# Interleaving input tiles and weight blocks one to one at the start of an eight-core hybrid layer

## The chip, the cores and the metric

The kernel runs on all 8 cores of one Trainium2 chip; each core does one prompt of 2048 tokens and 16 single-token samples. The metric is the device time in microseconds (us) of the slowest core, as the median of several executions. Some executions fall into a slower state in which the cores of one die show a lower granted TensorE clock (in the changed kernel's run of 851.31 us, 0.876 to 0.912 on the cores of one die and 0.985 to 0.995 on those of the other); they are left out.

Because the slowest core varies from run to run, I also use the mean span of the eight cores over the timed fast runs ("mean core"), and, from the profiled execution of each kernel, a count that I call **lost TensorE time**: time t minus the full-clock lengths of all matmuls that TensorE has started by t, averaged over the eight cores. The full-clock length is put at 0.4167 ns a column + 2.5 ns. That line gives 55.8, 145.8 and 215.8 ns for the bf16 matmuls of 128, 344 and 512 columns; in the trace of the kernel before the median distance between the starts of two of them is 56, 146 and 216 ns (396 of 344 columns take 57.77 us of its chain, 145.9 ns each, at a granted clock of 1.00). Matmuls of 16 columns come out too short: they start 25 ns apart in bf16 and 62 in fp32, where the count has 9 and 29; at the measured distances the gain of the change by 70 us would be 8.6 us instead of the 9.9 below, and the gain by 100 us the same 7.2. I counted the few fp32 matmuls with four times their columns, which is an assumption. That is too long for the fp32 ones of 128 columns, which start 109 ns apart in the trace, about twice the 56 of the bf16 ones; counted so, the rows of the tables rise by up to 2.4 us, but the gains of the change over the kernel before move by at most 0.5 us. A curve of lost time is worked out by me from the trace and isn't a view of the profile; tables marked "lost" hold it.

## The reference

```python
u = rmsnorm(x, norm_g)
lx, lg, sb, scg, sh, sg, q, qg, mg = split(u @ w_in)       # 1024 -> 8704 columns
xc = causal_dwconv4(lx) + b;  hs = rglru(xc)               # gated linear recurrence
z_a = (hs * silu(lg)) @ lru_wo
z_b = (silu(sg) * sb * causal_dwconv3(scg * sh)) @ sconv_wo
z_c = (attention(q, memory_k, memory_v) * silu(qg)) @ xa_wo
y   = x + (sigmoid(mg_a)*z_a + sigmoid(mg_b)*z_b + sigmoid(mg_c)*z_c) @ w_out
out = rmsnorm(y)             # and new states, memory keys and values
```

## The kernel before

The program isn't written in execution order. It builds a graph of tasks, and a planner at build time plays the tasks through with assumed durations and transfer times. That play fixes the order of the instructions on every engine, and the list is kept on the chip: on core 0 of the kernel before, ScalarE idles 10.57 us until 46.97 us over one evacuation, although the tiles that come next on its list had all landed by 41.3 us (the last was asked for at 25.1 us, and none took over 16.2 us). So an assumption in the planner never makes anything faster by itself, but it decides what stands behind what.

The parts that matter (cuts are marked with `# ...`):

```python
# an input tile of 128 tokens: load, square sum on ScalarE, 1/rms on GpSimd,
# scaling on VectorE (even tiles) or GpSimd (odd tiles), 8 transposes on TensorE, gain on VectorE
def p0(ti, src, nr, dst, gcols, tdst, prio):
    G.dma("sp", [(lambda: x_.ap[0:nr, :], src)], nr * 4096, [], [x_.tok], prio, None)
    G.act(... Square, accum_out=stat ...)
    rstd(ti, nr, prio)                       # two small GpSimd instructions
    # ... scale on DVE or Pool
    G.pe([tr(kc) for kc in range(KC)], 0.65, [xn_.tok, m_identb.t], [ps.tok], prio)
    G.dve(... dst = psum * gain ...)
for i in range(17):
    p0(i, src, nr, uT[:, :, i * 128:i * 128 + nr], pT[:, 0:8], t_uT[i], -100 + i)
for i in range(2):
    p0(17 + i, memp[...], ...)               # memory tokens
params()                                     # six small loads, early priority

# a weight block: 1024 x 128 columns, cast to bf16 by the DMA, issued by GpSimd
def wload(ap, prio):
    hw = Handle(w2ring if 2 <= state["nw"] < 6 else wring)
    t = G.dma("pool", [...], k * 65536 * 1.18, [], [hw.tok], prio, None)
    if state["nw"] >= 2:
        G.after(t, t_rs[min(16, state["nw"] + 1)])    # after the 1/rms of a tile
    state["nw"] += 1

# a projection of one block: 3 units of 688 columns, 16 matmuls of 344 columns each
def unit(lhs, nk, rhs, u, reads, prio, hold=()):
    G.pe([mm(k, b) for k in range(nk) for b in range(2)], ...)

# in the planner's play of a DMA
a, n = max(dmafree[q], end + 0.8), t.dma[1] / 250e3
fin = dmafree[q] + 1.3
# and among ready tasks: those within 0.4 us of the earliest compete by priority
```

A unit of 688 columns needs input tiles 0 to 5 (unit 0), 5 to 10 (unit 1), or 10 to 16 (unit 2).

The softmax here doesn't subtract the row's maximum and nothing guards it: scores larger than these inputs give would overflow.

## Time and profile before

| | before |
|---|---|
| median time | 781.86 us (three runs, 780.9 to 782.59) |
| mean core span | 777.5 us |
| TensorE busy | 93% of the span |

The first lines are from the page of the slowest core (core 0): busy time and instructions by engine, then busy tenths in 40 slices of 19.5 us, and the shares of the chain that ended last.

```profile
PE 726.6 (93%) x4884; PEld 460.6 (59%) x4884; DVE 395.2 (51%) x379; ACT 340.2 (44%) x404; POOL 247.5 (32%) x303
...
PE   2579998999999998999999999999999999999995
...
PEclk9979998999999999999999999999999999999998
DMA  8999921414242333242334595655896828226933
...
PE 85%; DMA 5%; issue 2%; ACT 2%; DVE 2%; POOL 2%; SPq 0%; POOLq 0%; ACTq 0%; DVEq 0%
```

TensorE (PE) is nearly full from the fourth slice on. The first three slices aren't, and the DMA engines (last row) are busiest there: the start is a phase of its own, bound by transfers, and the rest is bound by TensorE.

The DMA queues between 12 and 16 us (queue, packets, MB, share of the 16 engines): q1 carries the input tiles, q0 the weights.

```profile
q1 hardware_dynamic: 294, 1.08, 85.8%
q0 software_dynamic: 292, 0.07, 20.9%
```

The two queues send the same number of packets. A tile's packet is 4 KB, a weight's is 256 B as written, so the weights get about a sixteenth of the bytes (0.07 MB against 1.08). A block of 256 KB has 1024 packets and a tile of 512 KB 128: at equal counts one block lands per eight tiles. That the queues take turns packet by packet is my reading of the equal counts (294 and 292 here, 337 and 338 between 24 and 28 us); more than the counts the trace doesn't show.

What that does to the engines, on core 0. In the chain (start, length, what), and then by engine in order of time (start, length, engine, line, instruction, and in brackets the idle time before it with its releaser):

```profile
18.23 23.49 DMA R<-w_in
```

```profile
24.49 4.03 PE L761 MATMUL PP<-R 128*128 128x344 bf16 x16 [1.48 <-DVE R L674]
...
32.03 2.49 PE L761 MATMUL PP<-R 128*128 128x344 bf16 x16 [2.11 <-DMA R<-w_in]
...
42.13 4.75 PE L761 MATMUL PP<-R 128*128 128x344 bf16 x16 [7.16 <-DMA R<-w_in]
```

```profile
46.97 0.73 ACT L936 CAST R<-PP 128x688 bf16<-128x688 f32 x1 [10.57 <-PE PP L761]
```

```profile
38.22 0.95 POOL L133 DMA_DIRECT2D R<-w_in  x1
48.91 0.18 POOL L651 TENSOR_SCALAR R<-R 128x1 f32<-128x1 f32 x1 [9.75 <-ACT R L734]
...
51.70 0.96 POOL L133 DMA_DIRECT2D R<-w_in  x1
```

The third block, asked for at 18.23 us, arrives only when TensorE can start at 42.13. That stalls a convoy: ScalarE has the evacuation of that unit next in its list and idles 10.57 us; the row statistics of the next tiles stand behind it; GpSimd waits 9.75 us for those; and GpSimd is also the engine that asks for weight blocks, so none is asked for between 38.22 and 51.70 us. (The named releaser, line 734, is ScalarE's small parameter work just behind the statistics, which ended at 48.74.)

Lastly the projection matmuls alone, by stretch (stretch, its length, busy us and count, granted clock, DMA share, GB/s); the clock column reads 1.00 before the first clock record, though eight transposes take 1.01 us there and 0.61 us later:

```profile
core 0: us, PE busy (x), PEclk, DMA share, GB/s
0.00:40.00 40.00, 6.52 (x32) 0.97 0.98 259
40.00:50.00 10.00, 6.48 (x28) 0.59 1.26 114
50.00:70.00 20.00, 11.39 (x77) 1.00 0.83 89
70.00:100.00 30.00, 29.75 (x202) 1.00 1.02 116
100.00:140.00 40.00, 23.78 (x143) 0.91 0.22 41
140.00:360.00 220.00, 195.26 (x1310) 0.99 0.35 33
```

By 70 us core 0 has done 32 + 28 + 77 = 137 of 4104 projection matmuls, 20 us of work.

### The profile page before, as it was taken

What the parts mean: (1) busy time and instruction counts of PE and PEld (TensorE: products, weight loads), DVE (VectorE), ACT (ScalarE), POOL (GpSimd) and SP (SyncE); (2) the same over time, 40 slices, a digit from 0 to 9 for tenths busy, and PEclk for the clock granted to TensorE, in tenths of its full rate; (3) what the DMA queues carried; (4) which work ended last, traced back from release to release, by engine and by line L of the source; (5) the groups of instructions that cost most, each with busy time, mean ns of one, the idle gap of its engine ahead of it and who ended that gap; (6) DMA issues with size and microseconds to landing.
All of it is one profiled execution on the core that took longest, in us unless ns stands there. A gap on an engine that the chain in (4) does not pass through costs nothing.

```text
span 782.0 us, 13246 instructions; the slowest of 8 cores (776.0 to 782.0 us)
## 1 busy us (share of the span) xinstructions
PE 726.6 (93%) x4884; PEld 460.6 (59%) x4884; DVE 395.2 (51%) x379; ACT 340.2 (44%) x404; POOL 247.5 (32%) x303
## 2 busy tenths in 40 slices
PE   2579998999999998999999999999999999999995
PEld 1356654655655654666666666666666666665442
DVE  3544043265684863877875874546321221223665
ACT  4442358886759658676571211121212112112332
POOL 5845000121120210212114344435464454423221
PEclk9979998999999999999999999999999999999998
DMA  8999921414242333242334595655896828226933
GB/s 223 296 92 129 117 68 15 41 15 41 28 45 25 28 34 35 28 41 24 39 31 78 81 194 88 94 110 66 111 121 73 119 28 76 23 109 215 294 141 138
DMA packets 112618, 69.47 MB, mean 89 GB/s; under 512 B 93987, under 2 KB 100213, under 8 KB 112539
## 3 DMA queue, kind: packets, MB, share of 16 engines
q0 software_dynamic: 99808, 31.60, 39.3%
q1 hardware_dynamic: 12747, 37.03, 14.4%
q8 instruction: 40, 0.66, 0.4%
q14 instruction: 23, 0.19, 0.1%
HBM read 90.53 MB, written 9.82 MB: 128 GB/s over the span
## 4 chain that ended last, share of the span: by engine, by line
PE 85%; DMA 5%; issue 2%; ACT 2%; DVE 2%; POOL 2%; SPq 0%; POOLq 0%; ACTq 0%; DVEq 0%
PE PP L761 73%; PE PP L1189 8%; DMA R<-w_in 3%; PE PP L967 2%; DMA R<-xp 1%; PE PP L901 1%; ACT R L825 1%; PE PP L959 1%; DMA R<-cv 1%; POOL R L653 1%; PE PP L1053 1%; DVE R L839 1%; ACT R L962 1%; POOL R L663 0%; DVE R L1072 0%
## 5 line engine op out<-in xcount | busy, mean ns | idle before, releaser
L761 PE MATMUL PP<-R 128*128 128x344 bf16 x4104 | 616.5, 311 | 17.2 <-DMA R<-w_in 9.3
L761 PEld LDWEIGHTS PP<-R 128*128 128x128 bf16 x4104 | 400.1, 98 | 225.9 <-issue 28.2
L133 POOL DMA_DIRECT2D R<-w_in x68 | 61.7, 910 | 293.0 <-PE PP L761 266.3
L1141 ACT ACTIVATE R<-PP 128x688 f32<-128x688 f32 x72 | 53.6, 744 | 221.8 <-PE PP L761 197.8
L1150 DVE SCALAR_TENSOR_TENSOR R<-R,PP 128x688 f32<-128x688 f32 x72 | 62.5, 871 | 157.3 <-PE PP L761 134.5
L1189 PE MATMUL PP<-R 128*128 128x512 bf16 (+1 forms) x272 | 59.0, 379 | 0.0
L1154 POOL TENSOR_TENSOR R<-R 128x688 f32<-128x688 f32 x24 | 39.3, 1642 | 33.5 <-DVE R L1150 32.5
L812 DVE SCALAR_TENSOR_TENSOR R<-R 128x2048 f32<-128x2048 f32 x18 | 42.3, 2349 | 8.1 <-ACT R L809 7.0
L1189 PEld LDWEIGHTS PP<-R 128*128 128x128 bf16 (+1 forms) x272 | 26.4, 97 | 32.2 <-issue 0.4
L1159 POOL TENSOR_TENSOR R<-R 128x688 bf16<-128x688 f32 x24 | 38.9, 1642 | 17.7 <-DVE R L1150 17.5
L1198 ACT ACTIVATE R<-R 128x1024 f32<-128x1024 f32 (+1 forms) x17 | 18.0, 1057 | 46.3 <-DVE R L1193 46.3
L867 DVE TENSOR_TENSOR R<-PP,R 128x688 f32<-128x688 f32 x18 | 15.7, 874 | 31.0 <-PE PP L761 31.0
L1193 DVE SCALAR_TENSOR_TENSOR R<-PP,R 128x1024 f32<-128x1024 f32 (+1 forms) x17 | 20.8, 1224 | 20.6 <-PE PP L1189 20.6
L825 ACT ACTIVATE R<-PP,R 128x688 f32<-128x688 f32 x36 | 27.7, 833 | 6.4 <-PE PP L761 6.4
L674 DVE TENSOR_TENSOR R<-PP,R 128x1024 bf16<-128x1024 bf16 (+1 forms) x19 | 21.6, 1171 | 17.0 <-PE PP L671 16.5
L671 PE MATMUL PP<-R 128*128 128x128 bf16 (+1 forms) x152 | 13.7, 252 | 16.5 <-DVE R L663 12.7
L873 DVE SCALAR_TENSOR_TENSOR R<-R 128x2048 f32<-128x2048 f32 x12 | 28.2, 2347 | 0.9 <-ACT R L870 0.7
L651 POOL TENSOR_SCALAR R<-R 128x1 f32<-128x1 f32 (+1 forms) x36 | 7.5, 209 | 62.5 <-ACT R L1198 44.5
L839 DVE TENSOR_TENSOR_SCAN R<-R 128x2048 f32<-128x2048 f32 x6 | 26.5, 4422 | 0.4
L975 DVE TENSOR_TENSOR R<-PP,R 128x512 f32<-128x512 f32 x16 | 10.9, 688 | 29.3 <-ACT R L973 21.4
L1055 DVE TENSOR_TENSOR R<-R,PP 128x1024 f32<-128x1024 f32 x16 | 19.5, 1216 | 11.2 <-PE PP L1053 9.4
L936 ACT CAST R<-PP 128x688 bf16<-128x688 f32 x12 | 8.8, 730 | 35.1 <-PE PP L761 33.5
(129 smaller groups left out, 587.9 us busy)
## 6 DMA issues: line engine op xcount, KB each, us to landing
R<-w_in POOLq DMA_DIRECT2D x68, 256.0 KB, 5.1
R<-xp SPq DMA_DIRECT2D x32, 512.0 KB, 9.1
R<-ck SPq DMA_DIRECT2D x16, 512.0 KB, 4.2
y_p<-R SPq DMA_DIRECT2D x16, 512.0 KB, 2.8
R<-cv POOLq DMA_DIRECT2D x16, 256.0 KB, 7.2
R<-w_out POOLq DMA_DIRECT2D x8, 256.0 KB, 6.4
R<-xa_wo POOLq DMA_DIRECT2D x14, 128.0 KB, 4.1
R<-lru_wo POOLq DMA_DIRECT2D x8, 192.0 KB, 4.6
```

The costliest lines, as they stand in the source:

```text
L133: eng.dma_start(out=out, in_=in_).then_inc(sems[semkey], 16)
L674: G.dve(lambda e: e.tensor_tensor(out=dst, in0=ps.ap.bitcast(BF16)[:, 0:1024].rearrange("p (k t) -> p k t", k=KC)[:, :, 0:nr], in1=gcols.u ...
L761: return lambda e: e.matmul(ps.ap[:, b * 512:b * 512 + BLK], lhs(k), rhs[:, k, c:c + BLK], start=(k == 0), stop=(k == nk - 1))
L812: G.dve(lambda e, k=k: e.scalar_tensor_tensor(out=xc[:, 0:T], in0=lxp[:, k:k + T], scalar=cw(k), in1=xc[:, 0:T], op0=ALU.mult, op1=ALU.add ...
L825: G.act(lambda e, ps=ps, dst=dst, u=u, bcol=bcol: e.activation(out=cols(dst, u), in_=pv(ps), func=AF.Tanh, scale=0.5, bias=dv[:, bcol:bcol ...
L839: G.dve(lambda e: e.tensor_tensor_scan(out=xc[:, 0:T], data0=thr[:, 0:T], data1=thi[:, 0:T], initial=0.0, op0=ALU.mult, op1=ALU.add), T, t ...
L873: G.dve(lambda e, k=k: e.scalar_tensor_tensor(out=cy[:, 0:T], in0=cinp[:, k:k + T], scalar=sw(k), in1=cy[:, 0:T], op0=ALU.mult, op1=ALU.ad ...
L1141: G.act(lambda e, ps=pg[u], th_=th_: e.activation(out=b3(th_.ap), in_=pv(ps), func=AF.Tanh, scale=0.5), UW, [pg[u].tok], [th_.tok], Px - E ...
L1150: G.dve(lambda e, zp=zp, th_=th_, dst=dst: e.scalar_tensor_tensor(out=b3(dst.ap), in0=b3(th_.ap), scalar=1.0, in1=pv(zp), op0=ALU.add, op1 ...
L1154: G.pool(lambda e, acc=acc, th_=th_: e.tensor_tensor(out=acc.ap, in0=acc.ap, in1=th_.ap, op=ALU.add), 1.6, [acc.tok, th_.tok], [acc.tok], Px)
L1159: G.pool(lambda e, acc=acc, th_=th_, u=u, j=j: e.tensor_tensor(out=mT[:, j, u * UW:(u + 1) * UW], in0=acc.ap, in1=th_.ap, op=ALU.add), 1.6 ...
L1189: return lambda e: e.matmul(ps.ap[0:nr, b * 512:(b + 1) * 512], mT[:, k, c0:c0 + nr], wo[:, k, b * 512:(b + 1) * 512], start=(k == 0), sto ...
```

## The change

Its intent: let tiles and weights share the DMA engines evenly, so that TensorE finds work from the first tiles on. The core of the diff (moved code and priorities of the small parameter work are cut):

```diff
+def wload(ap, prio):                       # no longer tied to a tile's 1/rms, but:
+    if "pre" in state:
+        G.after(G.tasks[-1], state["pre"])  # behind the list of first blocks
+def unit(..., split=False):                 # start of the kernel: halves of 344 columns
+    if split:
+        for b in range(2):
+            t = G.pe([mm(k, b) for k in range(nk)], ...)
+            t.xgate = [t_tr[i] for i in range(17) if i * 128 < (u + 1) * UW] if b == 0 else []
+first = [C_Q, C_Q + 128, C_Q + 256, C_Q + 384, C_LG, C_SG, C_LX, C_SB, C_LG + 128, C_SCG, C_SH, C_SG + 128, C_LX + 128]
 for i in range(17):
+    if i >= 6:
+        wait = [w_toks[min(i - 5, len(w_toks) - 1)]]   # a tile waits for a weight block
+    elif i >= 3:
+        wait = [x_toks[i - 3]]                         # at most three tiles in flight
+    else:
+        wait = []
-    p0(i, src, nr, uT[...], pT[:, 0:8], t_uT[i], -100 + i)
+    x_toks.append(p0(i, src, nr, uT[...], pT[:, 0:8], t_uT[i], -100 + i, wait))
+    while len(w_toks) < len(first) and len(w_toks) <= i:
+        hw, lhs = wload(w_in_cols(first[len(w_toks)]), -100 + i)   # block i with tile i
+        if len(w_toks) >= 1:
+            G.after(G.tasks[-1], t_rs[i])
 # parameter and state loads: priority -88 -> 20 and -87 -> 25, after tiles 10 and 15
 # memory tokens: after the last block of the list
-        kv(pos)
+        kv(pos + KVP)                        # KVP = 10
-            if n < 4:
-                step(attend, n, d=14)
+            if 1 <= n < 5:
+                step(attend, n - 1, d=14)    # attention one gate stage later
-                sample_values(P - 5, 1.5)
+                sample_values(P - 5, 2.5)
 # planner: 250 -> 240 KB per us, landing 1.3 -> 2.3 us, tie window 0.4 -> 0.3 us
```

## The prediction

> **What bounds the kernel now.** TensorE: 726.6 of 782.0 us busy (the profile's first part), and the chain that ended last is 85% PE. A warm 128x344 matmul costs 146 ns (timeline). What is left is TensorE idling or running cold, and the table by windows puts most of it at the start. Up to 69.1 us TensorE did 128 projection matmuls (18.7 us warm), 152 input transposes (11.6 us at 76 ns) and the state transposes (2.3 us): 32.6 us of work, so about 36 us are lost. From 69 us on only some 16 us are idle in the whole run, plus about 8 us of output after the last matmul.
>
> **Why the start loses.** The chain shows one link of 23.5 us, "DMA R<-w_in": the third weight block, asked for at 18.2 us, lands after 41 us. The DMA view by 4 us windows shows the reason: while input tiles (4 KB packets, hardware queue) are queued, the weight queue (256 B packets) sends exactly as many packets: 294 against 292 in 12 to 16 us, 337 against 338 in 24 to 28 us. [...] A block has 1024 packets, a tile 128, so one block lands per eight tiles. Alone, a block needs about 1.9 us (2118 packets in 40 to 44 us). TensorE stands idle or at half clock from 34.9 to 46 us.
>
> **What the change does.** No work is removed. At most three tiles are in flight, and from the sixth on a tile waits for a weight block, so the weights get the engines. Estimated from the rates above: a tile 1.6 us, a block 1.9 us, a pair 3.5 us. First two blocks at about 15 and 17 us (seven or so blocks by 35 us; before, about two), tile 10 at about 33, the last tile at about 54 us (later than before, about 40), block 13 at about 55 us. First projection matmul at about 19 us (before 24.5). From 19 to 37 us TensorE gets a third-block (2.3 us) and a tile's transposes (0.6 us) per pair; from about 38 us, when tiles 6 to 10 are in, it has a backlog and should not idle until past 70 us. Loss in the start: 15 us ideally, 20 with cold matmuls and order errors: 16 us saved of the 36.
>
> Moved too: parameter and state loads come later, off the path. Attention shifts one gate stage later, so its stalls (122 to 133 us, ScalarE) move to later stages instead of vanishing. Keys and values: neutral. Wider spacing of the sample values: 1 to 2 us of the 557 to 576 us gap on this core, less on others.
>
> All saved start time lies on the critical path, as TensorE is nearly full afterwards. Minus 16 to 20 us, given back 1 to 2: about 764 us.
>
> **Predicted: 764 us**, 80% range 755 to 776. Faster by over 2% (under 766.2): 0.57; within 2%: 0.39; slower: 0.04.
>
> **What would show it.** Hardware packets well below software packets from 15 to 50 us; median weight landing in the start far under 20 us; no idle of TensorE over 4 us after 20 us; lost TensorE time in the first 70 us 15 to 22 us; from 140 us on the table by windows alike except shifted.
>
> **What would make it wrong.** TensorE's fixed order, planned from assumed transfer times, blocks on a late block or tile; evacuations wait for buffers shared with input tiles; the last tile's lateness; new attention and gate collisions.

## The result, and the profile after

| | before | after |
|---|---|---|
| median time | 781.61 us (4 runs) | 778.57 us (3 fast runs 777.24 to 779.0; a slow one of 851.31 left out) |
| ratio of the fast runs | | 0.9956 (95% interval 0.9936 to 0.9977) |
| mean core span | 777.5 us | 772.3 us |

A ratio is the mean time of one kernel's fast runs over that of the other's of the same rounds, so it isn't quite the ratio of the medians. The change is worth 0.4% of the slowest core and 0.7% of the mean core; 764 us had been forecast, with a range up to 776.

The page of the slowest core (core 4), the same rows as before:

```profile
PE 727.6 (94%) x4884; PEld 459.4 (59%) x4884; DVE 398.3 (51%) x379; ACT 344.8 (44%) x408; POOL 246.0 (32%) x303
...
PE   2887999989999989989999999999999999999995
...
PEclk9999999999999989989999999999999999999998
DMA  9998934422613322412333694655895848226833
```

The second slice of TensorE rose from 5 to 8, the third from 7 to 8; the fourth fell from 9 to 7. The dip has moved. The DMA queues between 24 and 28 us now:

```profile
q0 software_dynamic: 992, 0.25, 70.1%
q1 hardware_dynamic: 144, 0.52, 40.8%
```

Weights send seven times as many packets as tiles, where before they sent as many. Median time from issue to landing of a weight block: 8.4 us (core 4, the first 80 us) instead of 19.9 (core 0, the first 110 us). So the mechanism that the change aims at works. The first projection matmuls and then the place near 66 us, on TensorE:

```profile
24.50 9.51 PE L644 MATMUL PP<-R 128*128 128x344 bf16 x56
```

```profile
61.38 1.33 PE L644 MATMUL PP<-R 128*128 128x344 bf16 x8
66.40 0.61 PE L710 MATMUL PP<-R 128*128 128x128 bf16 x8 [3.69 <-POOL R L702]
66.85 3.66 PE L644 MATMUL PP<-R 128*128 128x344 bf16 x24
```

The first projection matmul starts at 24.50 us, as before (24.49), and at 66.40 TensorE has been idle for 3.69 us until a late input tile (line 710 is the transposes) is scaled. The chain shows the same two queues taking turns as the limit:

```profile
43.25 13.61 DMA R<-w_in
...
57.08 5.38 DMA R<-xp
```

The projection matmuls by stretch on core 4:

```profile
core 4: us, PE busy (x), PEclk, DMA share, GB/s
0.00:40.00 40.00, 13.69 (x83) 1.00 0.99 193
40.00:50.00 10.00, 8.89 (x60) 1.00 1.21 183
50.00:70.00 20.00, 12.72 (x84) 1.00 0.95 184
70.00:100.00 30.00, 24.22 (x148) 0.94 1.10 128
100.00:140.00 40.00, 33.50 (x228) 1.00 0.37 54
140.00:360.00 220.00, 186.24 (x1219) 0.97 0.33 31
```

Up to 50 us core 4 has done 143 of them, against 60 in the kernel before. Up to 70 us it is 227 against 137. But from 70 to 100 us it does only 148, against 202. (In that stretch it also has to do the state transposes and the memory keys and values, which the kernel before has partly behind it or still ahead.) Lost TensorE time, in which those other matmuls are counted as work:

| lost by (us) | 20 | 40 | 50 | 70 | 100 | 140 | 200 | 280 | 360 | 760 |
|---|---|---|---|---|---|---|---|---|---|---|
| before | 18.2 | 30.7 | 34.4 | 40.6 | 41.8 | 46.2 | 50.0 | 52.4 | 58.3 | 67.2 |
| after | 18.2 | 24.1 | 24.8 | 30.7 | 34.6 | 34.6 | 39.3 | 48.0 | 53.3 | 62.9 |
| gain | 0 | 6.6 | 9.6 | 9.9 | 7.2 | 11.6 | 10.7 | 4.4 | 5.0 | 4.3 |

So nothing is gained in the first 20 us, 9.6 us in the next 30, and some of it is given back twice: between 70 and 100 us, and between 200 and 280 us. (The 11.6 at 140 is a loan: the kernel before has its first attention stall at 120 to 140 us, the changed one has it later.)

Spans and granted clock of the fastest and slowest core, before and then after:

```profile
core 0: 782.0 us, clock 0.983
...
core 2: 776.0 us, clock 0.992
```

```profile
core 0: 770.2 us, clock 0.997
...
core 4: 777.0 us, clock 0.985
```

In these two runs the fastest core has a higher granted clock than the slowest, with the same instructions (0.992 against 0.983, 0.997 against 0.985). In the profiled run after, core 0 has no half-clock spell between its warm-up and the end, and core 4 has 17 us of them (granted clock 0.5). In such a spell 16 matmuls of 344 columns took 4.75 us (core 0 of the kernel before, from 42.13 us), and 2.49 us before it (from 32.03 us). Half clock for 17 us is an estimated 8.5 us of lost work, more than the 6.8 us between the two cores. The metric takes the unluckiest of eight.

### The profile page after: what moved, and what is told of

Same layout as the page of the kernel before. It is cut to its first block, busy times and chain, and to the rows that moved or that the text cites. A ratio compares the mean times of both kernels' runs of the same rounds, so it can differ in the third digit from the quotient of the medians.

```text
span 777.0 us, 13244 instructions; the slowest of 8 cores (770.2 to 777.0 us)
## 1 busy us (share of the span) xinstructions
PE 727.6 (94%) x4884; PEld 459.4 (59%) x4884; DVE 398.3 (51%) x379; ACT 344.8 (44%) x408; POOL 246.0 (32%) x303
## 4 chain that ended last, share of the span: by engine, by line
PE 84%; DMA 6%; ACT 3%; DVE 2%; issue 2%; POOL 1%; POOLq 0%; SPq 0%; ACTq 0%; DVEq 0%
PE PP L644 72%; PE PP L1211 8%; DMA R<-xp 3%; DMA R<-w_in 3%; PE PP L989 2%; ACT R L847 1%; PE PP L981 1%; DVE R L834 1%; PE PP L1075 1%; ACT R L984 1%; PE PP L1114 0%; POOL R L692 0%; POOL R L702 0%; ACT R L698 0%; PE PP L770 0%
## 5 line engine op out<-in xcount | busy, mean ns | idle before, releaser
L644 PEld LDWEIGHTS PP<-R 128*128 128x128 bf16 x4104 | 399.4, 98 | 216.1 <-issue 19.4
L1172 DVE SCALAR_TENSOR_TENSOR R<-R,PP 128x688 f32<-128x688 f32 x72 | 62.6, 871 | 151.1 <-PE PP L644 137.0
L1176 POOL TENSOR_TENSOR R<-R 128x688 f32<-128x688 f32 x24 | 39.4, 1641 | 36.8 <-DVE R L1172 35.9
L1211 PEld LDWEIGHTS PP<-R 128*128 128x128 bf16 (+1 forms) x272 | 26.4, 97 | 32.3 <-issue 0.4
L713 DVE TENSOR_TENSOR R<-PP,R 128x1024 bf16<-128x1024 bf16 (+1 forms) x19 | 22.3, 1175 | 23.2 <-PE PP L710 21.7
L847 ACT ACTIVATE R<-PP,R 128x688 f32<-128x688 f32 x36 | 27.4, 834 | 5.0 <-PE PP L644 4.9
L895 DVE SCALAR_TENSOR_TENSOR R<-R 128x2048 f32<-128x2048 f32 x12 | 28.2, 2346 | 0.9 <-ACT R L892 0.7
L698 ACT ACTIVATE R<-R 128x1024 bf16<-128x1024 f32 (+1 forms) x19 | 20.1, 1056 | 15.9 <-DMA R<-xp 15.7
L710 PEld LDWEIGHTS PP<-R 128*128 128x128 bf16 (+1 forms) x152 | 10.8, 110 | 25.6 <-issue 25.1
```

The costliest lines, as they stand in the source:

```text
L644: return lambda e: e.matmul(ps.ap[:, b * 512:b * 512 + BLK], lhs(k), rhs[:, k, c:c + BLK], start=(k == 0), stop=(k == nk - 1))
L710: return lambda e: e.transpose(ps.ap.bitcast(BF16)[:, kc * 128:kc * 128 + nr], xn_.ap[0:nr, kc * 128:(kc + 1) * 128], identb[0:nr, 0:nr])
L847: G.act(lambda e, ps=ps, dst=dst, u=u, bcol=bcol: e.activation(out=cols(dst, u), in_=pv(ps), func=AF.Tanh, scale=0.5, bias=dv[:, bcol:bcol ...
L895: G.dve(lambda e, k=k: e.scalar_tensor_tensor(out=cy[:, 0:T], in0=cinp[:, k:k + T], scalar=sw(k), in1=cy[:, 0:T], op0=ALU.mult, op1=ALU.ad ...
L1172: G.dve(lambda e, zp=zp, th_=th_, dst=dst: e.scalar_tensor_tensor(out=b3(dst.ap), in0=b3(th_.ap), scalar=1.0, in1=pv(zp), op0=ALU.add, op1 ...
L1176: G.pool(lambda e, acc=acc, th_=th_: e.tensor_tensor(out=acc.ap, in0=acc.ap, in1=th_.ap, op=ALU.add), 1.6, [acc.tok, th_.tok], [acc.tok], Px)
```

## The experiments

Each kernel is the changed kernel with one edit unless it says otherwise; all gave correct results, all were timed over five rounds beside the kernel before. The changed kernel itself was not timed again in these rounds: its figures are the three fast runs of the first session, and the kernel before, which stayed within 777.3 to 777.7 us, is what ties the sessions together. Lost time is from the profiled execution, the mean core and the median from the timed fast runs.

| run | lost by 40 | 50 | 70 | 100 | 360 | 760 | mean core | median | ratio to before |
|---|---|---|---|---|---|---|---|---|---|
| before | 30.7 | 34.4 | 40.6 | 41.8 | 58.3 | 67.2 | 777.5 | 781.6 | 1 |
| after | 24.1 | 24.8 | 30.7 | 34.6 | 53.3 | 62.9 | 772.3 | 778.6 | 0.9956 |
| e1 attention back | 24.4 | 25.4 | 31.3 | 35.5 | 55.6 | 64.5 | 773.5 | 777.8 | 0.9946 |
| e3 no tile waits | 31.2 | 31.6 | 34.1 | 35.9 | 55.1 | 64.5 | 776.7 | 780.5 | 1.0003 |
| e4 tie window | 23.9 | 25.4 | 32.9 | 37.6 | 58.8 | 68.8 | 777.1 | 780.9 | 0.9994 |
| e5 slower DMA in the plan | 23.3 | 26.0 | 30.8 | 35.1 | 51.5 | 61.2 | 771.0 | 774.7 | 0.9914 |
| e6 two tiles per block | 24.4 | 27.4 | 29.7 | 33.4 | 54.4 | 63.7 | 773.2 | 778.2 | 0.9953 |
| e7 parameters early | 24.4 | 25.5 | 30.6 | 34.3 | 52.1 | 61.6 | 772.0 | 776.3 | 0.9937 |
| e8 whole units | 25.6 | 28.2 | 31.0 | 34.3 | 54.4 | 63.8 | 772.9 | 778.4 | 0.9959 |
| e9 before, new plan numbers | 31.1 | 34.1 | 37.8 | 39.5 | 56.7 | 66.6 | 778.0 | 783.3 | 1.0025 |
| e10 first half unit early | 22.3 | 25.6 | 29.3 | 32.0 | 49.1 | 59.2 | 768.8 | 773.6 | 0.9900 |
| e11 keys, values back | 24.4 | 25.5 | 32.1 | 36.5 | 54.3 | 64.4 | 773.9 | 780.1 | 0.9991 |
| e12 state transposes spread | 24.7 | 25.7 | 31.5 | 35.4 | 55.2 | 64.5 | 773.6 | 777.4 | 0.9951 |
| e13 combined | 22.4 | 26.8 | 30.0 | 33.9 | 50.4 | 60.1 | 769.6 | 774.4 | 0.9910 |
| e14 list ahead alone | 30.2 | 31.7 | 33.4 | 35.8 | 52.4 | 62.3 | 773.3 | 778.8 | 0.9968 |
| e15 e10 without tile waits | 31.1 | 32.3 | 34.1 | 37.1 | 57.0 | 66.3 | 777.0 | 781.2 | 1.0006 |
| e16 two half units early | 21.9 | 25.1 | 29.4 | 33.2 | 50.8 | 60.9 | 769.4 | 773.1 | 0.9895 |

### How far the planned order alone moves the time (e4)

```diff
-                    if r <= m + 0.3:
+                    if r <= m + 0.4:
```

> A control: the changed kernel with only the tie window of its planner put back from 0.3 to 0.4 us, so that the order of many instructions differs for no physical reason. If the order alone decides a few us (rival to every one-part explanation here), the time moves by 3 us or more either way; if not, it stays within 2 us of 778.8. Its own plan is 4 us longer than that of the changed kernel, so 780 to 784 if the chip follows the plan.

Measured: the mean core rises by 4.8 us, the median by 2.3. Nothing physical was changed, so an edit anywhere in this kernel can move the mean core by some 5 us (this is one control; others might move it more) merely because the planner deals the instructions in another order. A difference of one or two us between two rows of the table is therefore no evidence for a cause; the rows are read by where their lost time parts, and by the trace at that place.

### The tile waits taken away (e3)

```diff
-            if i >= 6:   wait = [w_toks[min(i - 5, len(w_toks) - 1)]]
-            elif i >= 3: wait = [x_toks[i - 3]]
-            else:        wait = []
+            wait = []
```

> The changed kernel with all waits of input tiles on other tiles or weight blocks taken away, so that tiles are queued as early as their buffers allow; all else as changed. If packets of the two queues taken in turn are what starved the weights, the third to sixth weight blocks land about 20 us after their issue again (8.4 us in the changed kernel), hardware and software packets are equal in number from 12 to 36 us, TensorE idles 5 us or more in one piece before 50 us and the time is 782 to 790 us. Rival (the alternation is not what gained; the later parameter and state loads or the halved units are): within 2 us of the changed kernel's 778.8.

Measured: the packets are equal in number again. Between 24 and 28 us:

```profile
q1 hardware_dynamic: 305, 1.12, 84.0%
q0 software_dynamic: 306, 0.08, 25.9%
```

The median landing of a block is 22.2 us, TensorE idles 5.4 to 6.6 us in one piece before 34 us on every core, and by 40 us 31.2 us are lost, 7.1 more than in the changed kernel. So the starvation is real and the alternation removes it. But by 100 us the two kernels are 1.3 us apart. Without the waits all tiles are in early, the blocks then come with nothing beside them (from 40 to 44 us the weight queue sends 1077 packets and the tile queue none), and TensorE, whose every block is now worth 7 us of matmuls (48 of 145.9 ns), loses little more. With the waits, the weights come early and the last tiles late. The sum of transfers is the same, and it fills the DMA engines in both (share 0.98 and 0.99 up to 40 us, 1.18 and 1.21 from 40 to 50 us, each on its slowest core). The end time doesn't decide between my expectation and its rival. The five fast runs took 779.6 to 787.0 us: their mean, 782.1, is at the lower edge of what I expected, their median, 780.5, within the rival's 2 us of 778.8, and the mean core, 4.4 us above the changed kernel's, within what e4 allows for the order. What excludes the rival for the first 40 us are the packets and the loss; by 100 us 5.9 of the 7.2 us gained stand without the alternation.

### Two tiles for each block (e6)

```diff
-                wait = [w_toks[min(i - 5, len(w_toks) - 1)]]
+                wait = [w_toks[(i - 4) // 2]]
```

> The changed kernel with two input tiles instead of one let through per weight block from the sixth tile on. Theory A (after 50 us the late tiles are the limit: one to one gives the weights more than TensorE can use while it has no tiles): the last tile is transposed near 52 us instead of 66, the lost TensorE time between 50 and 100 us falls from 9.8 to 5 us or less with at most 2 us more lost before 50 us, and the mean core span falls by 3 to 5 us against the changed kernel (772.3). Rival (the order, not the tiles): tiles come early and the loss by 100 us stays at 34 to 36 us.

Measured: the last full tile is transposed at 56 us instead of 66, and the loss between 50 and 100 us falls from 9.8 to 6.0 us (33.4 - 27.4). So the late tiles are what cost the changed kernel after 50 us. But 2.6 us more are lost before 50 us, since the weights come later, and the mean core doesn't gain (773.2). Tiles and weights pay for each other: the expected 3 to 5 us were not there.

### Slower transfers in the plan (e5)

```diff
-                a, n = max(dmafree[q], end + 0.8), t.dma[1] / 240e3
+                a, n = max(dmafree[q], end + 0.8), t.dma[1] / 215e3
```

> The changed kernel with one number changed in its planner: transfers are assumed to run at 215 instead of 240 KB per us, so that the order of TensorE puts more matmuls ahead of late tiles. Nothing on the chip gets faster. Theory A (TensorE's fixed order waits on tiles planned too early, 5.9 us too early for tile 15): the loss between 50 and 100 us falls from 9.8 us to 4 to 6, the lag of TensorE behind its plan stays under 1 us at the start, and the time falls to 773 to 776 us. Rival (between 50 and 100 us TensorE has nothing else to do, the tiles themselves are the limit): loss and time unchanged within 2 us, the waits only sit elsewhere.

Measured: the time is as theory A expected (774.7 us), but not for its reason. The loss between 50 and 100 us is 9.1 us, hardly changed; the waits of TensorE for tiles stand in the plan now instead of coming as a surprise. The difference arises after 100 us (16.4 us lost from 100 to 360, against 18.7), in stages that the edit wasn't meant for. By e4 that is within what another order does. Theory A of this run fell.

### The other parts put back one by one (e1, e7, e8, e11)

e1 puts the attention steps back to the gate stage of before:

```diff
-            if 1 <= n < 5:
-                step(attend, n - 1, d=14)
+            if n < 4:
+                step(attend, n, d=14)
```

> The changed kernel with attention put back to the gate stage it had before (head n in stage n), nothing else. Theory A (the start is where the forecast failed, attention only moves its stalls): within 2 us of the changed kernel (777 to 781 us), TensorE time lost between 100 and 360 us 15 to 17 us instead of 18.7 (mean of cores 0 to 7), with the stall again near 115 to 140 us. Theory B (the attention shift ate the gain): 774 us or less, 4 us or more saved, as the losses between 240 and 340 us fall by 6 us and nothing comes in their place.

e7 puts the parameter and state loads, and the small work on them, back to their early priorities:

```diff
-  ... 42000, [], [m_prt.t], 20, "prt")
-  G.after(G.tasks[-1], t_xd[10])
+  ... 42000, [], [m_prt.t], -88, "prt")
-  ... 300000, [], [m_sin.t], 25, "sin")
-  G.after(t, t_xd[15])
+  ... 300000, [], [m_sin.t], -87, "sin")
   # and 30, 42, 44 -> -86, -85, -84 for the work on them
```

> The changed kernel with only the parameter and state loads, and the small work on them, put back to their early places. If moving them is what gained the 5.9 us by 100 us that the run without tile waits still has over the kernel before, the loss by 100 us rises from 34.6 to about 40 and the time to 782 to 784 us. If they are off the path (the prediction), within 2 us of the changed kernel.

e8 goes back to whole units:

```diff
-            return [unit(..., hold[u], prio < 60) for u in range(NU)]
+            return [unit(..., hold[u], False) for u in range(NU)]
```

> The changed kernel with projections in whole units of 688 columns again instead of halves. If the halves are what gained at the start, the loss by 50 us rises from 24.8 to 28 or more and the mean core span from 772.3 to 775 or more. If not, within 1.5 us.

e11 puts back the memory step and the spacing of the sample values:

```diff
-KVP = 10
+KVP = 0
-                sample_values(P - 5, 2.5)
+                sample_values(P - 5, 1.5)
```

> The changed kernel with the memory key and value step and the spacing of the sample values put back as before. Both theories of mine call these parts neutral: within 1.5 us of the changed kernel in the mean of the cores (772.3), loss by 100 us 34 to 35.5, loss from 540 to 600 us 4 to 5.5. If they carry the gain: 775 or more.

Measured: e1 brings the stall back to 120 to 140 us and takes it from 240 to 280; from 100 to 360 us it loses 20.1 us, more than the 15 to 17 expected and than the 18.7 of the changed kernel. The attention shift did not eat the gain. e7 is 0.3 us better in the mean core and 2.3 us in the median: moving the loads gained nothing, so they are off the path, as predicted. e8 loses 3.4 us more by 50 us, as its theory said, and has none of that left by 70. e11 is 1.6 us worse in the mean core, just over its bound and within what an order does; lost time between 540 and 600 us is 4.8 us against 4.2. None of these parts is where the forecast went.

### What earned the gain, then (e9 and e14)

e9 is the kernel before with the planner's three numbers of the change. e14 is the changed kernel without tile waits, with the parameters early, whole units, and attention, keys and values as before. What it keeps are those numbers, the list of 13 blocks ahead and what is queued behind it.

```diff
 # e9, on the kernel before
-                a, n = max(dmafree[q], end + 0.8), t.dma[1] / 250e3
+                a, n = max(dmafree[q], end + 0.8), t.dma[1] / 240e3
-                fin = dmafree[q] + 1.3
+                fin = dmafree[q] + 2.3
-                    if r <= m + 0.4:
+                    if r <= m + 0.3:
```

> The kernel before with only the three numbers of its planner that the change also alters (rate 240, landing 2.3 us, tie window 0.3): no transfer is moved by a rule, only the planned order. If a good part of the gain is the plan and not the alternation, the loss by 100 us falls from 41.8 by 3 us or more and the mean core span from 777.6 to 774.5 or less. If the alternation and the moved loads did it, within 1.5 us of the kernel before.

> The changed kernel with all undone but the list of 13 weight blocks loaded ahead, with later loads and the memory tiles behind it, and the planner's numbers: no tile waits, loads of parameters and state early, whole units, keys, values and attention as before. If the list ahead is what earned the 5.9 us, the loss by 100 us is 36 to 37.5 us and the mean of the cores 775 to 776.5; if it was the planner's numbers and the keys, as e9 (39.5) and e11 (+1.9) suggest, the loss is 39 or more and the mean 777 or more.

Measured: e9 loses 2.3 us less by 100 us than the kernel before and ends no earlier (mean core 778.0). e14 has lost 35.8 us by 100 us and its mean core is 773.3, both a little better than expected. That is 4.2 us below the kernel before and within 1.0 us of the whole change, without any tile waiting for a weight. Its losses start as high as before (30.2 by 40 us), but from 40 to 70 us it loses 3.2 us where the kernel before loses 9.9 and e9 6.7. GpSimd on its slowest core (core 6) asks for the last two blocks of the list here:

```profile
40.19 0.96 POOL L134 DMA_DIRECT2D R<-w_in  x1
...
42.08 0.95 POOL L134 DMA_DIRECT2D R<-w_in  x1
```

In the kernel before, GpSimd asked for its ninth block only at 51.70 us, after the eighth at 38.2. The stretch from 50 to 60 us in the kernel before, in e9 and in e14, each on its slowest core (stretch, its length, busy us and count of PE, PEld, DVE, ACT and POOL, granted clock, DMA share, GB/s; the share is the sum of the packets' times over that of 16 engines and can pass 1):

```profile
50.00:60.00 10.00, 8.02 (x75) 5.80 (x73) 6.94 (x11) 6.33 (x12) 8.74 (x13) 1.00 0.57 60
```

```profile
50.00:60.00 10.00, 9.31 (x88) 6.48 (x86) 8.06 (x12) 6.19 (x12) 8.62 (x14) 1.00 1.26 111
```

```profile
50.00:60.00 10.00, 9.30 (x85) 6.67 (x84) 7.48 (x8) 4.00 (x8) 5.75 (x8) 1.00 1.38 124
```

The DMA engines are fuller in e14, but in e9 as well: over the eight cores the share is 0.57 to 0.99 before, 1.23 to 1.34 in e9 and 1.33 to 1.42 in e14. Yet e9 still has the convoy: GpSimd asks for no block there from 40.7 to 48.6 us on any core (on core 0 from 39.5 to 51.7). It had asked for ten by then, where the kernel before had asked for eight on seven of its cores. So the gap in the requests is not the whole loss: of the 6.7 us that e14 loses less than the kernel before from 40 to 70 us, the planner's three numbers alone bring 3.2. The other 3.5 go with the list of 13 blocks; the two other kernels with the list and without waits also lose only 2.9 us (e3) and 3.0 us (e15) there. How much of this lasts to the end is not shown. e14 ends 4.2 us below the kernel before in the mean core, but e3 and e15 only 0.8 and 0.5, and e4 allows 4.8 us for the order alone.

### The half unit that may start after three tiles (e10, e15, e16)

```diff
 # e10: for the first block of the list and unit 0
-  t.xgate = [... if i * 128 < (u + 1) * UW] if b == 0 else []
+  t.xgate = [... if i * 128 < (c + BLK if early else (u + 1) * UW)] if b == 0 else []
 # e16: for the first two blocks.   e15: e10 and  wait = []  as in e3
```

> The changed kernel in which the first half unit of the first weight block may start when its own three input tiles are transposed, instead of six. The forecast put the first projection matmul at 19 us; the changed kernel has it at 24.5, as before, where it waits for the sixth tile and not for weights. If the six-tile rule is what held it, the first projection matmul starts by 20 us and the loss by 40 us falls from 24.1 to 22 to 23; rival (the first weight block lands late): it still starts after 23 us. Time: 0 to 3 us better by either, since one half unit is 1.2 us.

> The changed kernel with the first half unit allowed after three tiles (as e10) but without any tile waits (as e3). If the alternation is worth something only when an early weight block can be used: the first weight block lands near 24 us here, the first projection matmul starts after 23 us in spite of the looser rule, and the mean of the cores is 775 or more, 6 us or more above e10 (768.8). Rival (the looser rule alone made e10 fast): first matmul by 20 us and the mean below 772.

> As e10, but the first halves of the first two weight blocks may start after three tiles. The second block's half is another 1.2 us of work before the sixth tile, if its weights have landed (about 17 to 19 us by e10's times): loss by 40 us 21 to 22 instead of 22.3, mean of the cores 767.5 to 769 (768.8 in e10). If it is the order of the rest that made e10 fast and not the rule, this one falls back to 771 or more.

Measured in e10, on core 1 (TensorE):

```profile
18.59 1.01 PE L710 MATMUL PP<-R 128*128 128x128 bf16 x8 [1.44 <-POOL R L702]
19.39 2.49 PE L644 MATMUL PP<-R 128*128 128x344 bf16 x8
21.87 0.61 PE L710 MATMUL PP<-R 128*128 128x128 bf16 x8
```

The first projection matmul starts at 19.39 us, the figure of the forecast. The 8 matmuls take 2.49 us, cold; after them the next tile's transposes take 0.61 us instead of 1.01: the full clock also comes earlier, at 21 to 27 us over the cores instead of 26 to 29. By 40 us 22.3 us are lost instead of 24.1, as expected. The mean core is 768.8 us, 3.5 below the changed kernel and a little more than the 0 to 3 expected; the ratio to before is 0.9900 (0.9884 to 0.9915). e16 gives the same within the noise (0.9895, mean core 769.4).

But the place doesn't fit. By 50 us e10 has lost 25.6 us, more than the changed kernel's 24.8: six of its eight cores have a half-clock spell between 40.0 and 47.4 us, where the changed kernel has none, and on core 7 TensorE waits 1.51 us for a weight block just before its spell. The early start is paid back there. What e10 gains, it gains after 50 us (32.0 against 34.6 lost by 100 us, 49.1 against 53.3 by 360), where the new rule isn't at work. The three kernels with this rule and the tile waits (e10, e13, e16) have mean cores of 768.8 to 769.6 us; the nine others with the waits and the six-tile rule (after, e1, e4 to e8, e11, e12) 771.0 to 777.1. The groups don't overlap, but they are only 1.4 us apart, and by 50 us all three have lost more than the changed kernel (25.1 to 26.8). So e10 shows what held the first projection matmul; that the rule earned the 3.5 us is not shown, and a better order of the rest remains a rival.

e15 shows that the rule needs the waits:

```profile
20.05 2.45 PE L644 MATMUL PP<-R 128*128 128x344 bf16 x8 [0.71 <-DMA R<-w_in]
...
33.49 2.74 PE L644 MATMUL PP<-R 128*128 128x344 bf16 x9 [9.17 <-DMA R<-w_in]
```

Its first half unit runs at 20.05 us, against my expectation of a start after 23. But the second block keeps TensorE waiting until 33.49 us, 13 us later; I put that down to the equal packet counts that e3, also without waits, shows (305 against 306). The mean core is 777.0, 8.2 us above e10 and more than e4 allows for the order. So the alternation does pay here. Under the six-tile rule it was 4.4 us (e3); the difference between the two is within what an order does.

### The state transposes spread out (e12)

```diff
-            G.pe([trs(gi) for gi in range(18)], 1.8, [...], [h.tok], 42)
+            for p in range(3):
+                G.pe([trs(gi) for gi in range(6 * p, 6 * p + 6)], 0.6, [...], [h.tok], 42 + (6 if g0 else 0) + 2 * p)
```

> The changed kernel with the 36 small state transposes (2.5 us in one place) cut into six groups of six with projections between. In both kernels a half-clock spell of 3.4 us follows the place where the 36 stand together (69 to 73 us before, 85 to 89 us after), so the start's gain shrinks from 9.9 us at 70 us to 7.2 at 100. If the run of small matmuls causes the spell, it is gone on all eight cores and the loss from 80 to 100 us falls by 1.5 us or more; rival (it comes from anything else at that time): a spell near 85 us stays on most cores.

All matmuls by stretch on core 4, in the changed kernel and then in e12:

```profile
core 4: us, PE busy (x), PEclk, DMA share, GB/s
84.00:88.00 4.00, 4.00 (x26) 0.62 1.07 144
```

```profile
84.00:88.00 4.00, 4.00 (x32) 1.00 1.15 146
```

In the changed kernel five of eight cores have a half-clock spell that begins between 84.2 and 87.1 us, right after the 36 matmuls of 16 columns; in e12 none has one between 80 and 100 us. So the spell goes with the small matmuls in one block. The forecast of its worth failed: the loss from 80 to 100 us is 2.6 us against 2.9, not 1.5 less, and more is lost from 100 to 160 us; the end is no better. Another order again.

### A combination (e13)

e7 and e10 with a planner rate of 220.

> A version that might beat both: the changed kernel with the planner's rate at 220, parameter and state loads early as before, and the first half unit started after three tiles. If the parts add: mean of the cores 769 to 771 us, slowest core 773 to 775 us. If the planned order decides, anywhere from 771 to 778.

Measured: mean core 769.6, median 774.4, as forecast if the parts add, but no better than e10 alone. So they don't add beyond e10.

## Why the prediction was wrong, point by point

**Right: the mechanism in the queues.** The shares of packets, the starvation, and their end are as predicted (992 against 144 packets between 24 and 28 us, landing 8.4 us); e3 brings the starvation back by taking the waits away. TensorE has no idle over 4 us after 20 us, as forecast (the longest is 3.9 us).

**Wrong, and the step that failed: "First projection matmul at about 19 us" and "from about 38 us ... it has a backlog and should not idle until past 70 us", which gave "16 us saved of the 36".** By 70 us 30.7 us are lost where 15 to 22 were forecast, and 9.9 saved. The trace and e10 showed what stands in place of the first half. A unit may not start before its sixth tile is transposed, and those transposes came at 22.0 us before and 23.7 us after (VectorE had the last of that tile past 24 us in both), not at 18 to 19. GpSimd does the statistics of the tiles and asks for the weights in turn, and tiles are 2 to 3 us apart there (transposes at 16.39, 18.44, 21.72 and 23.82 us on core 1). I took the arrival of the weights as the limit where it was the tiles' processing under the six-tile rule; allowing three tiles gives the 19.4 us. Until 26 to 29 us TensorE also runs cold (eight transposes take 1.01 us at 23.82 us on core 1, 0.61 at 66.40 on core 4), so the loss by 40 us is 24.1 us, where I had 15 to 20 for the whole start. The sum was too small in itself: by 20 us 18.2 us are already lost, before and after, and 17.6 in e10, which starts as early as the forecast. So the late first matmul explains only 1.8 us of the miss by 40 us (24.1 against 22.3). Another 5.9 us go between 50 and 70 us, the next point.

**Wrong: the pace.** A pair was estimated at 3.5 us from tile and block rates measured apart. On core 1 of the profiled run SyncE asks for tile 6 at 19.2 us and for tile 15 at 55.7: nine pairs in 36.5 us, 4.1 us each. The last full tile was squared by ScalarE at 62.6 us on core 4, not in at 54. That is the second half of the failing step: the backlog of TensorE ran dry, 5.9 us were lost between 50 and 70 us, and e6 tied that to the tiles.

**Wrong in principle: that earlier weights are gained time.** I counted what weights gain and treated the later tiles as a risk. In this start, where the DMA engines are full (share 0.99 up to 40 us and 1.21 from 40 to 50, core 4), letting one stream in earlier made the other late: the last full tile was squared at 62.6 us, where e3 without the waits had every tile in by 43.9 us (the last asked for at 27.0, none over 16.9). Of 7.1 us that the waits earn by 40 us (after against e3), 1.3 are left by 100 us.

**Wrong in the base: why the kernel before loses.** I blamed the late blocks themselves. But 9.9 of its 40.6 us go between 40 and 70 us, behind the third block, and of these the planner's numbers take off 3.2 and the list of 13 blocks 3.5 more, without alternation. How much of the 5.2 us at the end comes from there is not shown: with the list and without waits e14 keeps 4.2, e3 and e15 only 0.8 and 0.5.

**Half right: that all of it lies on the critical path.** Of 9.9 us gained by 70 us, 7.2 are left by 100. The half-clock spell after the state transposes, which the kernel before has had by 73 us, comes after 84 us in the changed one; 3.4 us at half clock on five of eight cores are an estimated 1.1 of these 2.7 us, though e12, without the spell, lost only 0.3 us less there. Between 100 and 360 us the changed kernel loses 18.7 us against 16.5, so the attention stages give back 2.2 us, near the 1 to 2 predicted; e1 shows that putting them back doesn't help. At the end 4.3 (lost time) to 5.2 us (timed runs) are left in the mean core, and 3.4 in the mean of the slowest cores, probably as half-clock spells strike cores unequally.

**Open.** What earned the 5.2 us of the change, and the 3.5 us of e10 after 50 us, is not settled. How much of the last 2 us between rows is the part named and how much is the planner's order can't be told apart: e4 moved the mean core by 4.8 us without a cause. For the same reason it stays open why e3, with all other parts of the change, is 3.4 us slower than e14, without them.

## What to carry to other kernels

Before counting the gain of reordering loads, ask whether the DMA engines are full in that phase: here they were (share 0.99 up to 40 us), and the earlier stream was paid for by the later one: of 7.1 us earned by 40 us, 1.3 were left by 100. Look up the rule that says with how much data the busy engine may begin: here six tiles where three suffice (first projection matmul at 24.5 against 19.4 us). And count what is lost before that first moment, which no reordering behind it gives back. Look also at which engine issues the loads: if it also computes, a late load can stop the requests for the next ones, as it did from 38.2 to 51.7 us in the kernel before. And where a planner fixes the order, measure what a meaningless change of order does before you believe differences of that size.

## What these traces show of the queues and the clock

- In the kernel before, tiles and weights sent equal numbers of packets of unequal size: 294 of 4 KB against 292 of 256 B between 12 and 16 us. The eight 256 KB blocks that core 0 asked for in the first 40 us took 15 to 29 us to land, where the packets of one need an estimated 1.9 us alone (2118 packets in 4 us from 40 to 44 us, 1024 per block).
- In the changed kernel, where tiles and other blocks are under way beside it, the median landing of such a block is 8.4 us.
- In the changed kernel 36 matmuls of 16 columns in fp32, which start 62 ns apart and take 2.6 us, are followed by half clock for 3.4 us on five of eight cores, and by none when they are spread (e12). Whether it is that they are transposes or that they are small, no run here shows.
- In the profiled fast runs before and after, all eight cores had granted clocks of 0.983 to 0.997 over the span, and 396 matmuls of 344 columns took 57.77 us at a granted clock of 1.00. In a slow run of e15 (919.6 us) the cores of one die had 0.808 to 0.820.
